# Attention items of three kinds grouped into clusters of every second step, and two qk turns to a bank

## The chip, the cores and the metric

The kernel runs on one core of one Trainium2 chip. The metric is the device time of one execution in microseconds; the median of several runs counts. The engines are named as in the profile: PE is TensorE's matmul stream and PEld its weight loads, DVE is VectorE, ACT is ScalarE, POOL is GpSimd and SP is SyncE, which issues most transfers.

## The reference

The reference is one layer of an encoder over 1024 tokens of width 1024, in float32, with one sequence. Cut to what matters here:

```python
h = rms_norm(x, g_norm1) * (1 + sc1) + sh1          # sc1, sh1, ... from silu(c) @ w_ada
qa, ka, va, qb, kb, vb, gates = split(h @ w_in)     # 8 heads a, 12 heads b, each of 64 columns
qa, ka = rms_norm(qa), rms_norm(ka)                 # per head
o_a = neighbourhood_attention(qa, ka, va, rpb)      # 2-D windows of 8 x 16 on a 16 x 64 grid, with bias
qb, kb = partial_rotary(rms_norm(qb)), partial_rotary(rms_norm(kb))
for g, (win, dil) in enumerate(((128, 1), (512, 4), (2048, 16))):
    o_g, lse_g = dilated_window_attention(qb[g], kb[g], vb[g], win, dil)   # 4 heads each
o_b = sum over g of softmax(lse)_g * o_g
merged = sigmoid(gate_a) * (o_a @ w_proj_a) + sigmoid(gate_b) * (o_b @ w_proj_b)
x = x + gt1 * (merged @ w_o)
x = x + gt2 * swiglu(rms_norm(x, g_norm2) * (1 + sc2) + sh2)               # width 2816
```

A dilated window attends to positions at distances of 0, dil, 2 dil, ... up to win / 2 on either side, so with the tokens sorted by their remainder modulo dil it is a band or a block of a small matrix.

## The kernel before, in words

Each float32 product is made of three float32r matmuls (PASS, L126): the operands are split into a high and a low part, and high by high, high by low and low by high are summed in one bank. PE, ACT, DVE, POOL and SP work at once. The order of PE is the order of the program (the manual schedule for PE near the top of the function); the other engines' instructions are put in order by a planner that simulates the timeline from costs, with a raised priority for functions marked `@urgent` by their offset (PP is 100, QT, AQ, AT and AV are 0). What an instruction must wait for, in banks and tiles too, is worked out by the framework from the accesses.

The input projection and the attention lie in one loop over steps n from 6 to 91 (from L808). A unit is a pair of heads: units 0 and 1 are kind 0 (dilation 1), 2 and 3 kind 1 (dilation 4), 4 and 5 kind 2 (dilation 16), 6 to 9 kind 3 (the neighbourhood). A step is one block of 128 tokens of one unit (n = 8u + t): eight chunks of three matmuls with 384 columns each (proj_chunk, L292) sum q, k and v of that block into a bank of tag d. Then proj_post (L304 to L343) normalises: ACT squares and copies (L310, L311, L327 or L330), DVE reduces and scales (L313 to L315 with rstd at L118 to L123), POOL rotates (L322 to L325). From step 80 on the chunks are those of the gates (L599).

Between the fourth and the fifth chunk of a step stands its block of attention, for older tokens and units, in this order on PE:

- at_scores (L441): the scores of the items that are due, in two banks of tag s, one for each head; six matmuls an item, the two heads on the two halves of the array's rows. at_qk (L455, L456) then reduces on DVE with the mask added and the maximum taken, and ACT makes the exponentials P.
- at_pv (L482): the results of the items of two steps ago, from the turned P and v, into one bank of tag v. DVE copies them out (L485) and SP sends them to DRAM (L486).
- qk_turn (L350): the tokens of two steps ago are transposed, q and k each 128 x 128, into one bank of tag v (s for n under 10). ACT makes the high parts from it (L368 of q, L369 of k), DVE the low parts (L370 of q, L371 of k).
- at_turn (L467): P of the items of the step before is transposed, one bank of tag t for each head; ACT copies one (L473), DVE the other (L471).

There are four tags (t, v, d, s) with two banks of 128 x 512 float32 each. An item is up to 128 queries of one unit with one to three blocks of 128 keys: kind 0 has nine items (the first and the last with 64 queries and one block, the others with two blocks), kind 1 eight with two blocks, kind 2 eight with one, kind 3 eight with two or three. unit_items (L396) lists them with a slot; the loop puts an item of unit u - 1 on step 8u + 2 + slot (the dictionary ready), so that a step has one item, and two where kind 0's last two share slot 7. Such a step's items pass through the same pairs of banks one after the other.

Other work lies in the steps: ada_step (L279, L281, and L258 once in eight steps) for the second half of the modulation, t_piece (L640 to L646), the weight splits (L107 on ACT, L108 on POOL or DVE). After unit 5 the statistics are read back (combine_stats at step 61) and the three dilations are merged (combine_step, L559). The late gate products (gate_prod, L953 and L954 among its evacuations) come after the loop, then the output projection and the feed-forward (L1192, L1362).

Big tiles (4 KB a partition: v, wa2, rb, tp, oacc, gsig, w1m and the landing tiles of the start) share seven places.

Of the kernel before, what the change touches and what calls it, by code (L numbers as in the profile page):

```python
# [10 lines left out]
F32 = mybir.dt.float32  # L11
# [23 lines left out]
WARM = 40  # L35
XSQ = "avavaaaa"
# [5 lines left out]
def hybrid_layer(ctx: ExitStack, tc: tile.TileContext, x, colp, wada1, wada2, bada2, wqkv, wg, wpa, wpb,  # L42
# [95 lines left out]
    NBIG = 7  # L138
# [5 lines left out]
    land = [big("land") for _ in range(NBIG)]  # L144
    seq = [0]

    def landing():
        seq[0] += 1
        return land[(seq[0] - 1) % NBIG]

# [87 lines left out]
    def rope_tab():  # L238
        cs = ap_.tile([128, 4, 64], F32, tag="qn", bufs=5, name="cs").rearrange("p h (a b) -> p (h a) b", b=32)
# [64 lines left out]
    def proj_post(U, t):  # L304
        pd = U.pd[t]
        qn = ap_.tile([128, 4, 64], F32, tag="qn", bufs=5, name="qn")
# [39 lines left out]
    def qk_turn(U, t, tag="v"):  # L346
        qf = U.qn[t].rearrange("p h d -> p (h d)")
        pt = bank(tag)
# [47 lines left out]
    def unit_items(U):  # L396
# [48 lines left out]
    def at_qk(I, h):  # L445
# [3 lines left out]
        P = I.P[h] = ap_.tile([128, 384], F32, tag="p", bufs=4, name="P")  # L449
# [12 lines left out]
    def at_turn(I, h):  # L462
# [5 lines left out]
        PT = I.PT[h] = ap_.tile([128, 3, 128], F32, tag="pT", bufs=3, name="PT")  # L468
# [7 lines left out]
    def at_pv(I):  # L476
# [10 lines left out]
        if I.last:  # L487
            unit_out(U)

# [179 lines left out]
    def ada_rows(k):  # L669
# [10 lines left out]
        def copy():  # L680
            rowk[k] = ap_.tile([128, 384], F32, tag="p", bufs=4, name="rowk")[:, :256]
            nc.scalar.activation(rowk[k], pa[:, :256], AF.Copy)
# [122 lines left out]
    cur, prev, done = [], [], []  # L805
    raws = {}
    nextw = {}
    for n in range(6, 92):  # L808
# [24 lines left out]
        done, prev, cur = prev, cur, ready.pop(n, [])  # L833
# [692 lines left out]
```

## Time and profile before

Three runs took 1538.08, 1543.08 and 1542.0 us, a median of 1542.0. The profiled execution took 1540.34 us, of which the span that the trace shows is 1538.5.

| stretch of the span, us | what | PE busy, us | DVE busy, us | granted clock |
|---|---|---|---|---|
| 69 to 79.5 | steps 8 and 9 | 8.76 | 7.86 | 1.00 |
| 79.5 to 382 | steps 10 to 57, items of kinds 0 to 2 | 295.68 | 221.76 | 0.99 |
| 382 to 540 | steps 58 to 81, kind 3 | 153.89 | 138.83 | 1.00 |
| 540 to 640 | gates, the last items | 100.00 | 49.86 | 1.00 |
| 640 to the end | gates, merge, output projection, feed-forward | 889.69 | 641.22 | 1.00 |

To read the profile: a row of a group has the line, the engine, the operation, the tiles that it writes and reads, and the number of instructions. In a timeline the first column is the start and the second the time from that start to the end of the last of the merged instructions, in us; matmuls overlap in the pipeline, so their starts tell more than their lengths. In a list of waits stand the total, the number of times and the longest. In a row of a stretch stand its length, each engine's busy time with its instructions, the granted clock as a share of full speed, the busy share of the DMA engines and GB/s.

### The profile page before, as it was taken

How to read it: one execution, taken by the hardware profiler on the slowest of the kernel's cores; microseconds unless marked ns; L12 is line 12 of the kernel's file. 1: busy time of each engine (PE TensorE's matmuls, PEld its weight loads, DVE VectorE, ACT ScalarE, POOL GpSimd, SP SyncE). 2: the span in 40 equal slices, each digit the busy share in tenths (PEclk: the TensorE clock that was granted, in tenths of full speed). 3: DMA queues.
4: the chain of work that ended last, by engine and by line, in shares of the span. 5: the costliest groups of instructions: out<-in, count | busy, mean ns of one | idle time of the engine just before them, and what ended most of it. 6: DMA issues, size and time to landing. Idle time of an engine off the chain costs nothing. (4 is left out here: it accounts for less than half of the span.)

```text
span 1538.5 us, 24632 instructions
## 1 busy us (share of the span) xinstructions
PE 1513.6 (98%) x8156; PEld 1268.2 (82%) x8156; DVE 1109.3 (72%) x2428; ACT 671.3 (44%) x1719; POOL 531.8 (35%) x540
## 2 busy tenths in 40 slices
PE   9999999999999999999999999999999999999998
PEld 7988898988888877788888888888888888887886
DVE  6867786776889855466665497788767775599468
ACT  5555654555555453245532344233233333344442
POOL 0422331321000030001361211677777775104464
PEclk9999999999999999999999999999999999999999
DMA  9615355552354354833553235345443334798342
GB/s 366 231 47 177 106 160 163 172 170 83 104 149 131 107 172 138 299 120 117 171 169 139 86 105 179 112 135 178 156 132 103 107 111 131 256 357 284 104 151 103
DMA packets 158016, 241.67 MB, mean 157 GB/s; under 512 B 27312, under 2 KB 77360, under 8 KB 157120
## 3 DMA queue, kind: packets, MB, share of 16 engines
q1 hardware_dynamic: 156736, 235.90, 47.0%
q10 hardware_dynamic: 1152, 4.19, 0.7%
q8 instruction: 65, 1.06, 0.3%
q14 instruction: 63, 0.52, 0.1%
HBM read 179.89 MB, written 60.15 MB: 156 GB/s over the span
## 5 line engine op out<-in xcount | busy, mean ns | idle before, releaser
L107 ACT ACTIVATE whi<-raw 128x512 fp32r<-128x512 f32 (+1 forms) x348 | 205.0, 601 | 300.5 <-PE ps_s L1362 40.6
L108 POOL TENSOR_TENSOR wlo<-raw,whi 128x512 fp32r<-128x512 f32 (+2 forms) x133 | 168.9, 1282 | 473.1 <-ACT whi L107 323.8
L292 PE MATMUL ps_d<-whi,hT 128*128 128x384 f32 x1152 | 317.5, 343 | 1.3 <-ACT v L327 1.3
L108 DVE TENSOR_TENSOR wlo<-raw,whi 128x512 fp32r<-128x512 f32 (+1 forms) x215 | 184.3, 868 | 79.3 <-ACT whi L107 74.6
L292 PEld LDWEIGHTS ps_d<-whi,hT 128*128 128x128 f32 x1152 | 211.0, 188 | 7.0 <-ACT vs L330 2.6
L292 PE MATMUL ps_d<-wlo,hT 128*128 128x384 f32 x576 | 193.9, 337 | 0.4 <-POOL wlo L108 0.4
L292 PEld LDWEIGHTS ps_d<-wlo,hT 128*128 128x128 f32 x576 | 108.8, 189 | 0.7 <-POOL wlo L108 0.7
L107 ACT ACTIVATE whi<-ws 128x512 fp32r<-128x512 f32 x65 | 41.0, 631 | 123.9 <-DVE ws L1209 47.4
L1142 POOL TENSOR_TENSOR e<-e,c 128x512 f32<-128x512 f32 x44 | 68.2, 1549 | 66.3 <-DVE c L1272 40.3
L322 POOL TENSOR_TENSOR ra<-qn,rtab 128x64 f32<-128x64 f32 x48 | 16.8, 349 | 170.8 <-DVE qn L315 144.0
L456 ACT ACTIVATE P<-P,st 128x256 f32<-128x256 f32 (+2 forms) x100 | 46.1, 462 | 58.5 <-DVE st L455 58.5
L108 POOL TENSOR_TENSOR wlo<-m,whi 128x512 fp32r<-128x512 f32 x35 | 51.9, 1493 | 54.6 <-ACT whi L107 54.5
L599 PE MATMUL ps_d<-hT,whi 128*128 128x512 f32 x192 | 60.5, 396 | 0.0
L1192 PE MATMUL ps_v<-h2T,whi 128*128 128x512 f32 x192 | 59.3, 390 | 0.0
L1192 PE MATMUL ps_s<-h2T,whi 128*128 128x512 f32 x192 | 59.2, 390 | 0.0
L456 ACT ACTIVATE P<-P,sx 128x384 f32<-128x384 f32 (+1 forms) x64 | 37.1, 580 | 48.0 <-DVE sx L455 48.0
L441 PE MATMUL ps_s<-qk 64*128 64x256 f32 (+3 forms) x492 | 53.8, 321 | 3.3 <-DVE qk L371 2.0
L1192 PE MATMUL ps_d<-h2T,whi 128*128 128x512 f32 x184 | 56.9, 390 | 0.0
L313 DVE TENSOR_REDUCE ss<-sq 128x4 f32<-128x256 f32 x80 | 33.1, 414 | 32.6 <-ACT sq L310 32.5
L441 PEld LDWEIGHTS ps_s<-qk 64*128 64x128 f32 (+1 forms) x492 | 35.0, 182 | 25.2 <-issue 13.2
L482 PE MATMUL ps_v<-PT,v 128*64 128x128 f32 (+1 forms) x672 | 54.6, 284 | 0.8 <-DVE PT L471 0.8
L108 DVE TENSOR_TENSOR wlo<-ws,whi 128x512 fp32r<-128x512 f32 x45 | 49.4, 1098 | 8.2 <-ACT whi L107 8.2
(436 smaller groups left out, 3989.6 us busy)
## 6 DMA issues: line engine op xcount, KB each, us to landing
raw<-in_w_dram SPq DMA_DIRECT2D x139, 256.0 KB
ga_d<-e SPq DMA_DIRECT2D x77, 256.0 KB
raw<-ga_d SPq DMA_DIRECT2D x77, 256.0 KB
wa<-in_wada_dram SPq DMA_DIRECT2D x32, 512.0 KB
raw<-in_wqkv_dram SPq DMA_DIRECT2D x80, 192.0 KB
m<-in_w_dram SPq DMA_DIRECT2D x44, 256.0 KB
raw<-in_wg_dram SPq DMA_DIRECT2D x42, 256.0 KB
xt<-in_x_dram SPq DMA_DIRECT2D x16, 512.0 KB
```

The source lines that it names most:

```text
L107: nc.scalar.activation(hi[:, :n], r, AF.Copy)
L108: (eng or nc.gpsimd).tensor_sub(lo[:, :n], r, fview(hi[:, :n]))
L292: nc.tensor.matmul(pd[:, :384], tok(a, k, t), U.w[k][b][:, :384], start=(k == 0 and i == 0), stop=(k == KT - 1 and i == 2))
L313: nc.vector.tensor_reduce(ss, sq.rearrange("p (h d) -> p h d", h=4), axis=mybir.AxisListType.X, op=ALU.add)
L322: nc.gpsimd.tensor_tensor(v4(ra), v4(qn[:, :, 0:16]), tv(0, 0, 16), op=ALU.mult)
L441: nc.tensor.matmul(I.pS[h][:nq, :nk], U.qk[a][hs, I.q0:I.q0 + nq], U.qk[2 + b][hs, I.kb0 * 128:I.kb0 * 128 + nk], start=(i == 0), stop=(i ...
L456: nc.scalar.activation(P[:nq, :nk], P[:nq, :nk], AF.Exp, scale=-1.0, bias=nm, accum_out=sm)
L482: nc.tensor.matmul(po[hs, :nq], U.v[:, I.kb0 + i, hs], I.PT[h][:, i, :nq], start=(i == 0), stop=(i == nkb - 1))
L599: nc.tensor.matmul(st["p"], gw[i, br][j][a][:, kk * 128:(kk + 1) * 128], hT[b][:, k, hs], start=(k == 0 and q == 0), stop=(k == 7 and q == 2))
L1142: nc.gpsimd.tensor_mul(sg, sg, up)
L1192: nc.tensor.matmul(pb, w[p][:, k * 128:(k + 1) * 128], b[q][:, k], start=(k == 0 and i == 0), stop=(k == 3 and i == 2))
```

## The change

Up to step 57 (PAIRED is 58) the block of attention is made at odd steps only; the even steps have nothing but their projection. Items of kinds 0 to 2 no longer have a step of their own: they go into a list, and each odd step from 11 on takes from its head as many as have 512 keys together, over the border between two units too, as a Cluster. All scores of a cluster are written first, one item beside the other into the same two banks (cl_scores), then reduced and exponentiated item by item (cl_qk). One odd step later its P are transposed into one bank for each head and copied out in as few pieces as lie together (cl_turn); another odd step later all results go into one bank, are copied once and sent with one transfer for each unit (cl_pv). There are 50 such items and 21 clusters, at the odd steps from 11 to 47 and at 51 and 53.

The qk turns come two to an odd step, of the tokens of three and two steps ago. The two tiles of such a pair share one bank, the first in columns 0 to 255 and the second in columns 256 to 511, and qk_turn is called for the first and then for the second. Tiles of unit 0 are turned at steps 8, 9, 11 and 13. From step 58 on each step is as before.

For this there are seven tiles qn instead of five, four turned P instead of three, wider tiles for P, turned P and staging, and an eighth big tile (the landing tiles stay seven); the reserve for transfer descriptors is set to 1024 bytes a partition. The diff, without the changed sizes of rope_tab, proj_post, at_qk and the start:

```diff
+PAIRED = 58
-    NBIG = 7
+    NBIG, NLAND = 8, 7
-    land = [big("land") for _ in range(NBIG)]
+    land = [big("land") for _ in range(NLAND)]
-        return land[(seq[0] - 1) % NBIG]
+        return land[(seq[0] - 1) % NLAND]
...
-    def qk_turn(U, t, tag="v"):
+    def qk_turn(U, t, tag="v", pt=None):
-        pt = bank(tag)
+        if pt is None:
+            pt = bank(tag)
...
+            I.o = o
...
-        PT = I.PT[h] = ap_.tile([128, 3, 128], F32, tag="pT", bufs=3, name="PT")
+        PT = I.PT[h] = ap_.tile([128, 4, 128], F32, tag="pT", bufs=4, name="PT")
...
         nc.sync.dma_start(I.dst, st[:, :nq])
         if I.last:
             unit_out(U)
+    class Cluster:
+        def __init__(self):
+            self.items, self.keys = [], 0
+        def add(self, I):
+            I.c0 = self.keys
+            self.items.append(I)
+            self.keys += I.nkb * 128
+    def cl_scores(C):
+        C.pS = [bank("s") for _ in range(2)]
+        for I in C.items:
+            U, nq, nk = I.U, I.nq, I.nkb * 128
+            for i, (a, b) in enumerate(PASS):
+                for h in range(2):
+                    hs = slice(h * 64, h * 64 + 64)
+                    nc.tensor.matmul(C.pS[h][:nq, I.c0:I.c0 + nk], U.qk[a][hs, I.q0:I.q0 + nq],
+                                     U.qk[2 + b][hs, I.kb0 * 128:I.kb0 * 128 + nk], start=(i == 0), stop=(i == 2))
+    @urgent(AQ)
+    def cl_qk(C):
+        C.P = [ap_.tile([128, 512], F32, tag="p", bufs=4, name="P") for _ in range(2)]
+        for I in C.items:
+            nq, c = I.nq, slice(I.c0, I.c0 + I.nkb * 128)
+            for h in range(2):
+                nm, sm = I.U.st[:nq, I.item, h:h + 1], I.U.st[:nq, I.item, 2 + h:3 + h]
+                nc.vector.tensor_tensor_reduce(C.P[h][:nq, c], C.pS[h][:nq, c], I.masks[h], -1.0, 3.0e38,
+                                               ALU.add, ALU.min, nm)
+                nc.scalar.activation(C.P[h][:nq, c], C.P[h][:nq, c], AF.Exp, scale=-1.0, bias=nm, accum_out=sm)
+    @urgent(AT)
+    def cl_turn(C):
+        C.PT = []
+        for h in range(2):
+            pt = bank("t")
+            PT = ap_.tile([128, 4, 128], F32, tag="pT", bufs=4, name="PT").rearrange("p b q -> p (b q)")
+            C.PT.append(PT)
+            cuts = []
+            for I in C.items:
+                for i in range(I.nkb):
+                    c = I.c0 + i * 128
+                    nc.tensor.transpose(pt[:, c:c + I.nq], C.P[h][:I.nq, c:c + 128], ident[:I.nq, :I.nq])
+                    if cuts and cuts[-1][1] == c:
+                        cuts[-1][1] = c + I.nq
+                    else:
+                        cuts.append([c, c + I.nq])
+            for a, b in cuts:
+                if h:
+                    nc.vector.tensor_copy(PT[:, a:b], pt[:, a:b])
+                else:
+                    nc.scalar.activation(PT[:, a:b], pt[:, a:b], AF.Copy)
+    @urgent(AV)
+    def cl_pv(C):
+        po = bank("v")
+        n, outs = 0, []
+        for I in C.items:
+            U, nq = I.U, I.nq
+            for i in range(I.nkb):
+                for h in range(2):
+                    hs, c = slice(h * 64, h * 64 + 64), I.c0 + i * 128
+                    nc.tensor.matmul(po[hs, n:n + nq], U.v[:, I.kb0 + i, hs], C.PT[h][:, c:c + nq],
+                                     start=(i == 0), stop=(i == I.nkb - 1))
+            if outs and outs[-1][0] is I.o:
+                outs[-1][3] = n + nq
+            else:
+                outs.append([I.o, I.q0, n, n + nq])
+            n += nq
+        st = ap_.tile([128, 512], F32, tag="stg", bufs=3, name="stg")
+        nc.vector.tensor_copy(st[:, :n], po[:, :n])
+        for o, q0, a, b in outs:
+            nc.sync.dma_start(o[:, q0:q0 + b - a], st[:, a:b])
+        for I in C.items:
+            if I.last:
+                unit_out(I.U)
     def unit_out(U):
         if U.kind == 3:
...
-                ready.setdefault(8 * u + 2 + slot, []).append(I)
+                if I.U.kind < 3:
+                    waiting.append(I)
+                else:
+                    ready.setdefault(8 * u + 2 + slot, []).append(I)
-        done, prev, cur = prev, cur, ready.pop(n, [])
+        if n >= PAIRED:
+            done, prev, cur = prev, cur, ready.pop(n, [])
+        elif n % 2:
+            done, prev, cur = prev, cur, []
+            if waiting:
+                cur = [Cluster()]
+                while waiting and cur[0].keys + waiting[0].nkb * 128 <= 512:
+                    cur[0].add(waiting.pop(0))
+        else:
+            done = []
...
-        turns = [(units[0], tt) for tt in {8: (0, 1), 9: (2, 3), 10: (4,), 11: (5,), 12: (6,), 13: (7,)}.get(n, ())]
-        if 10 <= n <= 81:
-            turns.append((units[(n - 2) // 8], (n - 2) % 8))
+        turns = [(units[0], tt) for tt in {8: (0, 1), 9: (2, 3), 11: (4, 5), 13: (6, 7)}.get(n, ())]
+        if PAIRED <= n <= 81 or 9 < n < PAIRED and n % 2:
+            turns += [(units[m // 8], m % 8) for m in ((n - 2,) if n >= PAIRED else (n - 3, n - 2)) if m >= 8]
...
-        for I in cur:
-            at_scores(I)
-            at_qk(I, 0)
-            at_qk(I, 1)
-        for I in done:
-            at_pv(I)
-        for q in turns:
-            qk_turn(*q, "s" if n < 10 else "v")
-        for I in prev:
-            at_turn(I, 0)
-            at_turn(I, 1)
+        if n >= PAIRED or n % 2 or n < 10:
+            for I in cur:
+                if I.__class__ is Cluster:
+                    cl_scores(I)
+                    cl_qk(I)
+                else:
+                    at_scores(I)
+                    at_qk(I, 0)
+                    at_qk(I, 1)
+            for I in done:
+                (cl_pv if I.__class__ is Cluster else at_pv)(I)
+            for j, q in enumerate(turns):
+                if j % 2 == 0:
+                    pq = bank("s" if n < 10 else "v")
+                qk_turn(*q, "v", pq[:, 256 * (j % 2):256 * (j % 2) + 256])
+            for I in prev:
+                if I.__class__ is Cluster:
+                    cl_turn(I)
+                else:
+                    at_turn(I, 0)
+                    at_turn(I, 1)
...
-    nc = _bacc.Bacc("TRN2", target_bir_lowering=False, num_devices=1)
+    nc = _bacc.Bacc("TRN2", target_bir_lowering=False, num_devices=1, dynamic_dma_scratch_size=1024)
```

More of the change, by code (lines that the diff above doesn't have):

```diff
@@ L238, in rope_tab @@
     def rope_tab():
-        cs = ap_.tile([128, 4, 64], F32, tag="qn", bufs=5, name="cs").rearrange("p h (a b) -> p (h a) b", b=32)
+        cs = ap_.tile([128, 4, 64], F32, tag="qn", bufs=7, name="cs").rearrange("p h (a b) -> p (h a) b", b=32)
         nc.sync.dma_start(cs, rope)
@@ L305, in proj_post @@
         pd = U.pd[t]
-        qn = ap_.tile([128, 4, 64], F32, tag="qn", bufs=5, name="qn")
+        qn = ap_.tile([128, 4, 64], F32, tag="qn", bufs=7, name="qn")
         U.qn[t] = qn
@@ L448, in at_qk @@
         pS = I.pS[h]
-        P = I.P[h] = ap_.tile([128, 384], F32, tag="p", bufs=4, name="P")
+        P = I.P[h] = ap_.tile([128, 512], F32, tag="p", bufs=4, name="P")
         if U.kind < 3:
@@ L680, in copy @@
         def copy():
-            rowk[k] = ap_.tile([128, 384], F32, tag="p", bufs=4, name="rowk")[:, :256]
+            rowk[k] = ap_.tile([128, 512], F32, tag="p", bufs=4, name="rowk")[:, :256]
             nc.scalar.activation(rowk[k], pa[:, :256], AF.Copy)
@@ L805, in hybrid_layer @@
     cur, prev, done = [], [], []
+    waiting = []
     raws = {}
```

## The prediction

> **What bounds the kernel now.** I read the page first, for the engine that has no room left.
>
> ```profile
> span 1538.5 us, 24632 instructions
> PE 1513.6 (98%) x8156; PEld 1268.2 (82%) x8156; DVE 1109.3 (72%) x2428; ACT 671.3 (44%) x1719; POOL 531.8 (35%) x540
> ```
>
> PE is busy for 98% of the span, so time is won or lost only where PE's own stream becomes shorter or longer. A measurement of this kernel can tell some 0.3% from no change, 4.6 us.
>
> Then the busy time by stretch: the steps 10 to 57, which the change regroups, run from 79.5 us to about 383 us, the steps 8 and 9 just before.
>
> ```profile
> core 0: us, PE busy (x) PEld busy (x) DVE busy (x) ACT busy (x) POOL busy (x), PEclk, DMA share, GB/s
> 79.50:382.00 302.50, 295.68 (x2027) 262.36 (x2028) 221.76 (x792) 171.26 (x647) 80.08 (x193) 0.99 0.44 134
> ```
>
> Here too PE is the bound (295.68 of 302.50 us). The waits of PE from 69 to 382 us show how little idleness there is to take away:
>
> ```profile
> PE ps_s L441 <- DVE qk L371: 2.0, 1, 2.0
> PE ps_d L292 <- ACT v L327: 1.3, 1, 1.3
> PE ps_s L441 <- DVE st L455: 1.2, 2, 0.6
> PE ps_t L467 <- ACT PT L473: 0.9, 2, 0.5
> PE ps_v L482 <- DVE PT L471: 0.8, 2, 0.4
> ```
>
> What is left is how PE strings its instructions together. The timeline of PE around one block of attention in the middle of a step, and a later block with three key blocks:
>
> ```profile
> 158.76 0.33 PE L292 MATMUL ps_d<-wlo,hT 128*128 128x384 f32 x1
> 158.94 0.34 PE L292 MATMUL ps_d<-whi,hT 128*128 128x384 f32 x1
> 159.21 0.62 PE L441 MATMUL ps_s<-qk 64*128 64x256 f32 x6
> 159.76 0.66 PE L482 MATMUL ps_v<-PT,v 128*64 128x128 f32 x8
> 160.34 0.44 PE L350 MATMUL ps_v<-ident,qn 128*128 128x128 f32 x2
> 160.62 0.60 PE L467 MATMUL ps_t<-ident,P 128*128 128x128 f32 x4
> 160.98 0.43 PE L292 MATMUL ps_d<-whi,hT 128*128 128x384 f32 x1
> 161.24 0.34 PE L292 MATMUL ps_d<-wlo,hT 128*128 128x384 f32 x1
> ...
> 428.34 0.88 PE L482 MATMUL ps_v<-PT,v 128*64 128x128 f32 x12
> 429.15 0.44 PE L350 MATMUL ps_v<-ident,qn 128*128 128x128 f32 x2
> 429.42 0.82 PE L467 MATMUL ps_t<-ident,P 128*128 128x128 f32 x6
> 430.00 0.43 PE L292 MATMUL ps_d<-whi,hT 128*128 128x384 f32 x1
> ```
>
> Matmuls overlap, so the distance of the starts counts. A projection matmul takes 0.18 us (158.76 to 158.94). The block takes 161.24 - 158.94 = 2.30, less two such distances (0.35): 1.95 us.
>
> **Term 1: half as many blocks.** The number of PE instructions stays the same; 48 blocks (steps 10 to 57) become 24. A second item in a block costs only its marginal price. Results: 12 matmuls take 0.81 (428.34 to 429.15) where 8 take 0.58, so eight more cost 0.46. Turns of P: six take 0.58 where four take 0.36, so 0.11 each, 0.44 for four; the two transposes of a second qk turn 0.22 at the same price. Six more scores: no row shows two items back to back in one bank; between 0.35 (the 0.058 of a result matmul, which also runs in pairs on half the array) and the full 0.55 (159.21 to 159.76). I take 0.35, because the block's entry is in the 0.55. Sum 1.47, so a double block takes 3.42 against 3.90 and each pair of steps gains 0.48: 24 x 0.48 = 11.5 us (with 0.55 for the scores 6.7). Items of kind 2 have one key block each; I let them gain the same.
>
> **Term 2: waits that lose their reason.** In the steps with two items of kind 0 the second item waits for banks that the first still holds (L455 1.2, the turned P 0.9 + 0.8); in clusters they share the bank. The 2.0 us is a unit's first scores behind its last qk turn one step earlier; now two steps lie between. Together 4.9 us. That longest wait also cost clock:
>
> ```profile
> 238.00:243.00 5.00, 3.04 (x22) 2.52 (x21) 4.64 (x16) 2.21 (x6) 0.00 (x0) 0.80 0.09 26
> 243.00:249.00 6.00, 6.00 (x39) 5.45 (x38) 4.25 (x18) 2.43 (x11) 1.74 (x7) 0.88 0.91 240
> ```
>
> The lost part is 0.20 x 5 + 0.12 x 6 = 1.7 us. Next late after them would be the projection's bank (L292 behind L327, 1.3), which the change leaves. I take 7 us, between 3 and 9.
>
> **Term 3: a wait that is new.** The qk turns now go two to a bank: the transposes of tile a into columns 0 to 255, then ScalarE (L368, L369) and VectorE (L370, L371) read them, and only then, in program order, come the transposes of tile b into columns 256 to 511. In the kernel before every turn has a bank for itself, so no row shows PE writing one half while another engine reads the other. The nearest rows are those of readers. L370 needs what L368 wrote and reads columns 0 to 127; L369 reads columns 128 to 255 and its result is nothing to L370. Yet L370 waits for it (the tile qk, 69 to 382 us, what it was released by and who waited):
>
> ```profile
>   ACT qk L369: 6.2, 15
> ...
>   DVE qk L370: 6.7, 16
> ```
>
> A second place is the late gate products, where L954 copies a bank into its own half of a tile and uses nothing that L953 made, but L953 reads the same bank:
>
> ```profile
> L954 ACT ACTIVATE sg<-ps_t x1: 601/601/601, 711.7 to 711.7; 128x512 f32<-128x512 f32 x1
> ...
>   DVE sg L953: 1.4, 1
> ```
>
> So in this program two engines at one bank are ordered even when their columns differ and both only read. A write by PE into a bank that is being read should be no freer: tile b's transposes wait until L371 of tile a has ended. The Trainium skill ("PSUM — Partial Sum Buffer", section "PSUM bank collisions raise a hardware error") says that engines must be kept apart by bank and quadrant of partitions and not by address. By that rule the wait is there and the sum is the one below; by addresses alone it is that of the first rival. The two rows agree with the rule; that PE's writes obey it too no run here shows yet.
>
> The size of the wait, from when tile b's transposes could start (0.28 after tile a's, 160.34 to 160.62) to the end of L371, in three steps of before:
>
> ```profile
> 162.64 0.28 DVE L371 TENSOR_TENSOR qk<-ps_v,qk 128x128 fp32r<-128x128 f32 x1
> 248.84 0.44 PE L350 MATMUL ps_v<-ident,qn 128*128 128x128 f32 x2
> 249.75 0.42 DVE L471 COPY PT<-ps_t 128x256 f32<-128x256 f32 x1 [0.41 <-PE ps_t L467]
> 250.35 0.28 DVE L371 TENSOR_TENSOR qk<-ps_v,qk 128x128 fp32r<-128x128 f32 x1
> 274.60 0.44 PE L350 MATMUL ps_v<-ident,qn 128*128 128x128 f32 x2
> 277.47 0.27 DVE L371 TENSOR_TENSOR qk<-ps_v,qk 128x128 fp32r<-128x128 f32 x1
> ```
>
> 162.92 - 160.34 - 0.28 = 2.30; 250.63 - 248.84 - 0.28 = 1.51; 277.74 - 274.60 - 0.28 = 2.86. The mean is 2.2. I take 2.0, because the copy of the turned P (L471, 0.42) that VectorE makes ahead of L371 in the second of these steps can't be there: PE reaches the turns of P only after this wait. Against a smaller value, VectorE has four score reductions before the turn where it had two. The ends for the range are 1.1 (the shortest less that copy) and 2.9 (the longest). Queued behind the waiting transposes are the turns of P of the cluster before, the second half of the step's projection and all of the next step's, and behind those ScalarE's squares of the projection. Nothing covers it, since PE is the bound.
>
> How often: the 56 tiles of units 0 to 6 make 28 pairs (steps 8 and 9 one each, 11 and 13 two each, 15 to 57 one in each of 22 odd steps). 28 x 2.0 = 56 us.
>
> Waits of this length can also cost clock. The 2.0 us idle at 240 us was followed by the 0.80 and 0.88 above; an idle of 1.7 us later was not:
>
> ```profile
> L559 PE MATMUL ps_t<-ident,fb 128*128 128x128 f32 x4 | 0.7, 287 | 1.7 <-ACT PT L473 1.7
> 434.00:438.00 4.00, 3.90 (x34) 3.50 (x34) 3.17 (x14) 1.34 (x7) 0.00 (x0) 1.00 0.60 166
> ```
>
> I let two of the 28 do so: 2 x 1.7 = 3.4 us. The Trainium skill ("TensorE: Matmul & The Clock Gate", Part 1, on the HAM clock gate) has the clock halved after an idle window of some 3.4 us, and the window free-running. The 2.0 us shows that less idleness can do it here; the third rival is where it does so often.
>
> **At nothing.** The score reductions and exponentials come in fours instead of twos; their results are needed a pair of steps later, so the projection in between hides them, and what could be exposed (VectorE's queue ahead of L370) is in term 3's ends. Copies of turned P and of results become fewer and wider on engines that are not the bound (VectorE 221.76 of 302.50). The result transfers leave SP in fewer pieces and up to a pair of steps later, but unit 5's last results come at step 57 instead of 59, before the statistics are read at step 61, and no transfer stands in PE's waits. The eighth big tile, seven qn tiles, the wider P, PT and staging tiles and the smaller descriptor reserve move addresses, not work. If smaller reserves slowed transfers, weight splits would come late; the DMA share of 0.44 leaves room for that.
>
> **Sum.** Against the profiled execution (1540.34 us, its span 1538.5): 1540.3 - 11.5 - 7 + 56 + 3.4 = 1581.2. That execution lies 1.7 us under the median of 1542.0, so 1583 us.
>
> **Rivals.** (1) The halves of a bank are independent for PE: tile b's transposes go on at once, and terms 1 and 2 stand alone: 1540.3 - 18.5 + 1.7 = 1523.5. For it: no row shows PE itself held back that way; against it, L370's 16 waits and L954's. This is the faster side. (2) The wait exists but is nearly covered: it pays back terms 1 and 2 at 18.5 / 28 = 0.66 us a pair, 1542. For it: the planner that orders ScalarE and VectorE may put the four reads first; against it, the shortest of the three is 1.51, and 1.1 without the copy. (3) The waits are longer and half of them halve the clock: 28 x 2.4 = 67, 14 x 1.7 = 24, so 1540.3 - 18.5 + 67 + 24 + 1.7 = 1614.5. For it: the 2.0 us at 240 did; against it: 1.7 us at 434 did not.
>
> **Chances.** Forecast 0.72, for waits of 1.1 to 2.9 us (28 x 1.1 = 31 with term 2 at 9 and no clock lost gives 1552.5, 28 x 2.9 = 81 with terms 1 and 2 at 6.7 and 3 gives 1617); rival 1 0.10; rival 2 0.05, split 0.02 faster, 0.02 same, 0.01 slower; rival 3 0.13. So faster 0.12, same 0.02, slower 0.86. The range holds the forecast's ends and the middle of rival 3, and leaves out rivals 1 and 2 and the longer half of rival 3: 1553 to 1620.
>
> **What would show it.** Right: in the list of PE's waits a new largest entry, L350 behind L371, some 28 times for about 56 us, and PE busy clearly under 98%; a block of two items 3.4 us long apart from that wait; L441 behind L371 and behind L455 gone; granted clock under 1.00 in a few windows. Wrong: no such entry (rival 1), or one of less than 0.7 us each (rival 2). A long new wait of PE elsewhere, on transfers for instance, would mean that I looked at the wrong place.

## The result, and the profile after

The changed kernel takes 1624.88 us, the median of six runs (1618.99 to 1627.43), against 1540.41 for the kernel before, also of six (1537.82 to 1543.08). The ratio is 1.055, with a 95% interval from 1.0532 to 1.0567. The direction and the mechanism are those of the prediction, but the time lies 42 us above 1583 and just beyond the upper end of the range, 1620.

The profiled execution took 1627.35 us. By the change the lines have moved: the projection is L293, the transposes of a qk turn L352, ScalarE's two reads of them L370 and L371, VectorE's two L372 and L373. In the clusters L511 are the scores, L521 and L523 the reductions and exponentials, L536 the turns of P, L556 the results and L564 their copy. From the page, the span, the busy time, the granted clock in 40 slices and two groups:

```profile
span 1625.5 us, 24441 instructions
PE 1538.7 (95%) x8156; PEld 1301.9 (80%) x8156; DVE 1109.7 (68%) x2374; ACT 670.8 (41%) x1694; POOL 532.2 (33%) x540
PEclk9989898998999999999999999999999999999999
...
L293 PE MATMUL ps_d<-whi,hT 128*128 128x384 f32 x1152 | 329.9, 359 | 0.0
...
L352 PE MATMUL ps_v<-ident,qn 128*128 128x128 f32 x152 | 35.0, 317 | 66.9 <-DVE qk L373 53.6
```

PE makes the same 8156 matmuls but is busy 25.1 us longer (1513.6 before), and its idle time has grown too, from 24.9 to 86.8 us. So there are two losses, PE waiting and PE working more slowly. The first third of the clock row dips below 9 several times. The idle time stands ahead of the transposes of the qk turn (66.9 us). By stretches, first the steps 8 to 57 (which took 315.50 us before, with 306.93 busy) and then all the rest:

```profile
core 0: us, PE busy (x) PEld busy (x) DVE busy (x) ACT busy (x) POOL busy (x), PEclk, DMA share, GB/s
68.20:472.80 404.60, 332.85 (x2105) 306.50 (x2104) 231.16 (x783) 180.61 (x646) 86.26 (x212) 0.89 0.35 109
472.80:1625.50 1152.70, 1141.24 (x5567) 937.14 (x5565) 829.73 (x1451) 450.04 (x942) 434.93 (x301) 1.00 0.47 153
```

All of the loss lies in the steps that were regrouped, 89.1 us. The rest took 1154.90 us before. From here on "the stage" means the steps 8 to 57. PE's waits in it, with the total, the number and the longest:

```profile
PE ps_v L352 <- DVE qk L373: 53.6, 21, 6.2
PE ps_v L352 <- POOL rb L325: 8.8, 3, 3.0
PE ps_v L352 <- POOL qn L326: 4.6, 2, 2.6
PE ps_s L352 <- DVE qk L373: 4.5, 2, 2.6
```

The four rows are the 28 waits between the two tiles of a pair, 71.5 us. Five of them are put down to POOL, whose instruction happened to end last. It belonged to the rotation of a later tile: counted in order, tile b's own rotation (L326) had ended 2.6 us or more before PE went on, in all 24 pairs that have one. In the instructions of all 28 PE starts again 0.06 to 0.15 us after the end of L373. One of these five, in the timeline of PE, ScalarE and VectorE:

```profile
225.82 0.49 ACT L523 ACTIVATE P<-P,st 128x256 f32<-128x256 f32 x1
225.99 0.44 PE L352 MATMUL ps_v<-ident,qn 128*128 128x128 f32 x2
226.29 0.41 DVE L564 COPY stg<-ps_v 128x256 f32<-128x256 f32 x1
226.31 0.39 ACT L523 ACTIVATE P<-P,st 64x128 f32<-64x128 f32 x1
...
226.70 0.49 ACT L523 ACTIVATE P<-P,st 128x256 f32<-128x256 f32 x1
...
227.19 0.35 ACT L370 ACTIVATE qk<-ps_v,hg 128x128 fp32r<-128x128 f32 x1
227.44 0.26 ACT L371 ACTIVATE qk<-ps_v 128x128 fp32r<-128x128 f32 x1
227.73 0.35 DVE L372 SCALAR_TENSOR_TENSOR qk<-ps_v,hg,qk 128x128 fp32r<-128x128 f32 x1 [0.51 <-ACT qk L371]
228.00 0.28 DVE L373 TENSOR_TENSOR qk<-ps_v,qk 128x128 fp32r<-128x128 f32 x1
...
228.42 0.41 PE L352 MATMUL ps_v<-ident,qn 128*128 128x128 f32 x2 [1.99 <-POOL qn L326]
```

Tile a is transposed by 226.43. ScalarE is still at the exponentials of the block's own scores and comes to L370 at 227.19. VectorE has been through its reductions and a copy, waits for L371, and L373 ends at 228.28. Then tile b is transposed. Over the 28 waits (1.30 to 6.17 us, median 2.19, mean 2.55) the parts are, in the mean: 1.00 us until ScalarE begins L370, 0.56 for L370 and L371, 0.30 until VectorE begins L372, 0.57 for L372 and L373, 0.12 until PE goes on. In the longest, 6.17 us, VectorE began L372 3.24 us late, because work ahead of it on its queue (L282, L721) waited for transfers.

The slower work is seen in the stretches ahead of and behind two waits, each 3.41 us:

```profile
211.73:215.14 3.41, 1.62 (x13) 1.66 (x14) 1.55 (x8) 2.73 (x12) 0.00 (x0) 1.00 0.29 47
215.14:218.56 3.42, 3.42 (x22) 3.42 (x21) 1.29 (x5) 2.13 (x6) 0.00 (x0) 1.00 0.90 239
225.39:228.80 3.41, 1.42 (x20) 1.04 (x15) 2.34 (x12) 2.27 (x10) 1.05 (x4) 1.00 0.93 256
228.80:232.22 3.42, 3.42 (x16) 3.42 (x15) 1.89 (x5) 1.13 (x3) 0.00 (x0) 0.50 1.09 379
```

The wait of 1.82 us in the first row (1.79 of it inside the row) left the clock alone; the one of 1.99 in the third was followed by 3.4 us at half clock, in which PE made 16 matmuls where the second row has 22. The record of the granted clock has 17 such stretches in the stage, of 3.4 or 6.8 us, 92 us together; before it had one of 3.4.

### The profile page after: what moved, and what is told of

The parts are those of the page before. It is cut to its first block, busy times and chain, and to the rows that moved or that the text cites. A ratio compares the mean times of both kernels' runs of the same rounds, so it can differ in the third digit from the quotient of the medians.

```text
span 1625.5 us, 24441 instructions
## 1 busy us (share of the span) xinstructions
PE 1538.7 (95%) x8156; PEld 1301.9 (80%) x8156; DVE 1109.7 (68%) x2374; ACT 670.8 (41%) x1694; POOL 532.2 (33%) x540
## 5 line engine op out<-in xcount | busy, mean ns | idle before, releaser
L109 POOL TENSOR_TENSOR wlo<-raw,whi 128x512 fp32r<-128x512 f32 (+2 forms) x133 | 174.3, 1320 | 501.7 <-ACT whi L108 316.8
L293 PE MATMUL ps_d<-whi,hT 128*128 128x384 f32 x1152 | 329.9, 359 | 0.0
L293 PEld LDWEIGHTS ps_d<-whi,hT 128*128 128x128 f32 x1152 | 227.3, 203 | 5.2 <-issue 2.6
L293 PE MATMUL ps_d<-wlo,hT 128*128 128x384 f32 x576 | 203.7, 354 | 0.4 <-POOL wlo L109 0.4
L293 PEld LDWEIGHTS ps_d<-wlo,hT 128*128 128x128 f32 x576 | 117.0, 203 | 0.7 <-POOL wlo L109 0.7
L352 PE MATMUL ps_v<-ident,qn 128*128 128x128 f32 x152 | 35.0, 317 | 66.9 <-DVE qk L373 53.6
L352 PEld LDWEIGHTS ps_v<-ident,qn 128*128 128x128 f32 x152 | 16.3, 150 | 80.5 <-issue 42.3
L311 ACT ACTIVATE sq<-ps_d 128x256 f32<-128x256 f32 x74 | 28.2, 382 | 112.7 <-PE ps_d L293 109.7
L523 ACT ACTIVATE P<-P,st 128x256 f32<-128x256 f32 (+2 forms) x100 | 45.3, 455 | 41.8 <-DVE st L521 41.8
L1244 ACT ACTIVATE e<-e 128x512 f32<-128x512 f32 x44 | 27.4, 630 | 72.5 <-DVE e L1379 47.2
```

Source lines behind the costliest of these rows:

```text
L109: (eng or nc.gpsimd).tensor_sub(lo[:, :n], r, fview(hi[:, :n]))
L293: nc.tensor.matmul(pd[:, :384], tok(a, k, t), U.w[k][b][:, :384], start=(k == 0 and i == 0), stop=(k == KT - 1 and i == 2))
L311: nc.scalar.activation(sq, pd[:, :256], AF.Square)
L352: nc.tensor.transpose(pt[:, i * 128:(i + 1) * 128], qf[:, i * 128:(i + 1) * 128], ident)
L523: nc.scalar.activation(C.P[h][:nq, c], C.P[h][:nq, c], AF.Exp, scale=-1.0, bias=nm, accum_out=sm)
```

## The experiments

Theory at this point: PE is made to wait with tile b while anything still reads tile a in the same bank; that wait is 2.55 us long 28 times, and its idleness halves the clock after most of them. The rivals were that the clusters themselves (wider tiles, fours of reductions, the smaller reserve) cost something, and that the order on ScalarE, not the bank, makes the wait as long as it is. Each experiment was timed beside the kernel before on the same chip (medians of 1534.93 to 1537.54 us), so ratios are compared. "Idle" is the length of the stage less PE's busy time in its row, "slower" is that busy time less that of the first experiment, whose matmuls are the same.

### Both tiles transposed before either is read

qk_turn is called in two parts, for the transposes and for the four reads.

```diff
-            for j, q in enumerate(turns):
-                if j % 2 == 0:
-                    pq = bank("s" if n < 10 else "v")
-                qk_turn(*q, "v", pq[:, 256 * (j % 2):256 * (j % 2) + 256])
+            for j in range(0, len(turns), 2):
+                pq = bank("s" if n < 10 else "v")
+                for part in ("write", "read"):
+                    for i, q in enumerate(turns[j:j + 2]):
+                        qk_turn(*q, "v", pq[:, 256 * i:256 * i + 256], part)
```

> The changed kernel with one thing altered: of each pair of qk turns both tiles are transposed before either is read, still in one shared bank. Theory (the loss is PE waiting for tile a's four reads before it may write tile b's columns, and the half clock that follows): L352 behind L373 vanishes from PE's waits (56.5 us in the changed kernel), the granted clock of 69 to 471 us goes from 0.89 to 0.99 or more, and terms 1 and 2 stand alone: 1519 to 1528 us. Rival (the clusters themselves, their later scores and their bursts on VectorE, cost the time): PE's waits move to other lines and the time stays above 1590 us.

Measured: 1522.50 us against 1534.93, 0.9918 (0.9903 to 0.9932), as expected. The bank is still shared; only the order has changed. Its busy time, its stage, and PE around a full block:

```profile
PE 1500.1 (99%) x8156; PEld 1269.1 (83%) x8156; DVE 1101.4 (72%) x2374; ACT 666.5 (44%) x1694; POOL 536.8 (35%) x540
```

```profile
67.90:365.20 297.30, 293.27 (x2104) 272.25 (x2104) 224.94 (x780) 172.71 (x645) 91.85 (x211) 0.99 0.47 145
```

```profile
217.90 0.34 PE L293 MATMUL ps_d<-whi,hT 128*128 128x384 f32 x1
218.17 0.98 PE L514 MATMUL ps_s<-qk 64*128 64x256 f32 x12
219.08 1.09 PE L559 MATMUL ps_v<-PT,v 128*64 128x128 f32 x16
220.10 0.66 PE L353 MATMUL ps_v<-ident,qn 128*128 128x128 f32 x4
220.60 1.04 PE L539 MATMUL ps_t<-ident,P 128*128 128x128 f32 x8
221.39 0.42 PE L293 MATMUL ps_d<-whi,hT 128*128 128x384 f32 x1
221.65 0.33 PE L293 MATMUL ps_d<-wlo,hT 128*128 128x384 f32 x1
```

The four transposes go in one piece (L353 here), and the idle time of the stage is 4.0 us. So the wait is a matter of order, not of sharing. This version beats both kernels. Against it the loss of the changed kernel divides: the stage is 404.60 - 297.30 = 107.3 us longer, of which 67.7 is idle time (71.75 against 4.03) and 39.6 slower work (332.85 against 293.27).

### One part alone: paired turns without clusters, clusters without paired turns

The first puts each item back on its own step and keeps two turns to a bank; the second keeps the clusters and gives each turn its own step and bank.

```diff
-        if n >= PAIRED:
-            done, prev, cur = prev, cur, ready.pop(n, [])
...
+        done, prev, cur = prev, cur, ready.pop(n, [])
```

> The changed kernel without clusters: every item has its own step and its own banks as in the kernel before, and only the qk turns come in pairs that share a bank, at odd steps. Theory: the same 28 waits and half clocks without what the clusters gain, so 1630 to 1650 us, slower than the changed kernel by 10 to 20 us. Rival (the clusters cost the time): within 10 us of the kernel before.

```diff
-        if PAIRED <= n <= 81 or 9 < n < PAIRED and n % 2:
-            turns += [(units[m // 8], m % 8) for m in ((n - 2,) if n >= PAIRED else (n - 3, n - 2)) if m >= 8]
+        if 10 <= n <= 81:
+            turns.append((units[(n - 2) // 8], (n - 2) % 8))
...
-                qk_turn(*q, "v", pq[:, 256 * (j % 2):256 * (j % 2) + 256])
+                qk_turn(*q, "s" if n < 10 else "v")
```

> The changed kernel with the clusters, but each qk turn in its own step and with a bank of its own, as in the kernel before. Theory: no wait of PE behind L373, and most of the gain of the clusters less the turns' separate places at even steps: 1524 to 1536 us. Rival (the clusters, or the wider tiles and the smaller descriptor reserve, cost the time): above 1590 us.

Measured: pairs alone 1618.19, 1.0541 (1.0526 to 1.0557), below the 1630 to 1650 that was expected; clusters alone 1524.98, 0.9928 (0.9912 to 0.9945), as expected. Pairs alone, the two largest rows of PE's waits between the tiles of a pair, and the stage:

```profile
PE ps_v L352 <- DVE qk L373: 46.1, 24, 3.7
PE ps_s L352 <- DVE qk L373: 6.1, 2, 3.5
```

```profile
68.10:464.60 396.50, 335.43 (x2093) 296.72 (x2092) 230.46 (x819) 184.40 (x669) 85.67 (x211) 0.93 0.36 112
```

The pairs bring a loss of the same size (1.0541 against 1.055) without any cluster: idle 61.1 us, and 28.5 of slower work against the kernel before (335.43 against 306.93). It is less than was expected of them, because their 28 waits are shorter: 2.03 us in the mean against 2.55, with 0.35 against 1.00 until ScalarE begins L370. The clusters cost nothing and bring nearly all of the gain that the first experiment shows. That rival is out.

### The wait filled with work of no use

Twenty transposes of the identity, into a bank that nothing reads, stand between the two tiles of a pair.

```diff
                 if j % 2 == 0:
                     pq = bank("s" if n < 10 else "v")
+                elif n < PAIRED:
+                    pf = bank("t")
+                    for i in range(20):
+                        nc.tensor.transpose(pf[:, :128], ident, ident)
```

> The changed kernel with 20 more transposes of the identity (0.11 us each at full clock, 2.2 us) between the first and the second tile of each pair, into a bank that nothing reads: PE is kept busy while it would wait. Theory that idleness halves the clock and that this is the larger part of what the prediction missed: the granted clock of the steps 8 to 57 rises from 0.89 to 0.98 or more, the wait before L352 shrinks to below 20 us in all, and although 560 transposes are added the time falls to 1590 to 1612 us. Rival (the clock costs nothing that the waits do not cost already): 1625 us or more.

Measured: 1596.83, 1.0402 (1.0387 to 1.0418), as expected. Its stage:

```profile
67.80:444.40 376.60, 359.60 (x2665) 336.05 (x2664) 230.79 (x782) 180.33 (x646) 86.95 (x211) 0.99 0.38 117
```

The 560 fillers start 0.109 us apart, 61 us in all, and 17.0 us are still idle: 78 us in which PE does nothing for the result, more than the 71.75 of the changed kernel. Yet the stage is 28.0 us shorter. What has gone is slower work, 359.60 - 61 - 293.27 = 5.3 us instead of 39.6. So idleness, and not the transposes or the bank, costs the clock.

### A raised priority for the turns

```diff
-PP, QT, AQ, AT, AV = 100, 0, 0, 0, 0
+PP, QT, AQ, AT, AV = 100, 100, 0, 0, 0
```

> The changed kernel with the qk turns' instructions raised in the planner's priority to that of the projection's (QT from 0 to 100), so that ScalarE and VectorE read tile a ahead of the cluster's exponentials and copies. Theory (the wait is 2.55 us and not 2.0 because up to four exponentials stand ahead of L370 on ScalarE): the 28 waits shrink to 1.4 to 1.9 us each, fewer of them halve the clock, and the time falls to 1570 to 1605 us. Rival (the wait is the chain of the four reads itself): 1615 us or more.

Measured: 1621.08, 1.0538 (1.0522 to 1.0554). The expectation failed. The 28 waits are in the mean what they were (2.55 us, with 0.99 until ScalarE begins L370), because the order on ScalarE is the same: the exponentials still stand ahead of L370. Why the raised priority did not move them, no run shows.

### The same order, a bank for each tile

```diff
-            for j, q in enumerate(turns):
-                if j % 2 == 0:
-                    pq = bank("s" if n < 10 else "v")
-                qk_turn(*q, "v", pq[:, 256 * (j % 2):256 * (j % 2) + 256])
+            for q in turns:
+                qk_turn(*q, "s" if n < 10 else "v")
```

> The changed kernel, its order on PE unchanged, but the two tiles of a pair each take the next bank of tag v, as every turn did in the kernel before. Theory (the bank is what is waited for): L352 no longer waits for L373; in its place tile b waits for VectorE's copy of the cluster's results out of the other v bank (L564), some 0.4 to 0.9 us, 22 times: 1530 to 1548 us, granted clock 0.99 or more. Rival (the order of the two tiles on PE costs it, whatever the banks): above 1600 us.

Measured: 1575.34, 1.0239 (1.022 to 1.0259), between the two expectations. PE's longest waits and the stage:

```profile
PE ps_v L352 <- DVE stg L564: 36.4, 19, 4.7
PE ps_v L352 <- DVE qk L373: 5.0, 2, 3.5
```

```profile
68.00:421.00 353.00, 308.94 (x2103) 283.73 (x2103) 229.56 (x782) 177.82 (x646) 88.36 (x211) 0.95 0.40 123
```

The wait on L373 goes (the two that are left are the steps with four tiles for two banks), and another takes its place: tag v has two banks, the results of the cluster (L556) fill one just before tile a takes the other, so tile b needs the bank that VectorE still has to copy out (L564). It is 1.9 us long, 19 times, not the 0.4 to 0.9 that was expected.

### Work of use put into the wait

First the turns of P go between the two tiles; then those and three chunks of the projection, for 24 of the 28 pairs.

```diff
                 if j % 2 == 0:
                     pq = bank("s" if n < 10 else "v")
+                else:
+                    p_turns()
                 qk_turn(*q, "v", pq[:, 256 * (j % 2):256 * (j % 2) + 256])
```

> The changed kernel with the turns of P of the cluster before moved between the two tiles of the pair. Theory: 0.8 us of useful work cover a part of each wait, so the 28 waits keep 1.5 to 1.9 us of idleness in all but the longest, and idleness of that length halves the clock only sometimes: 1560 to 1595 us. Rival (any wait at this place halves the clock, whatever its length): above 1600 us.

```diff
+                if j % 2 and n > 9 and (n > 13 or j == 3):
+                    late.append((q, half))
...
         chunk()
         chunk()
         chunk()
+        if n > 9 and n % 2 and n < PAIRED:
+            for q, half in late:
+                qk_turn(*q, "v", half)
         chunk()
```

> The changed kernel with the turns of P and three chunks of the projection (0.8 and 1.6 us) between the two tiles of the pair, for 24 of the 28 pairs; the shared bank and the order of writing and reading stay. Theory (a wait costs only what is not covered): what remains are the 4 pairs of the steps 8 to 13 and the longest of the others, 10 to 20 us, so 1528 to 1550 us and a granted clock of 0.97 or more in the steps 8 to 57. Rival (the sharing costs by itself, by the array's or the bank's own slowness): above 1590 us.

Measured: 1593.29, 1.0362 (1.0344 to 1.038), and 1550.71, 1.009 (1.0063 to 1.0117), the one near the end of what was expected and the other just above it. The two stages:

```profile
68.00:440.10 372.10, 312.30 (x2104) 286.79 (x2103) 229.17 (x783) 179.71 (x646) 87.08 (x212) 0.94 0.38 117
```

```profile
67.90:400.50 332.60, 303.26 (x2105) 277.01 (x2104) 225.40 (x781) 176.12 (x646) 90.43 (x212) 0.97 0.42 130
```

With the turns of P between, the idle time is 59.8 us, 12.0 less than in the changed kernel, and the slower work 19.0 us, 20.6 less: waits that are a sixth shorter halve the loss of clock. With the projection as well 29.3 and 10.0 us are left, where 10 to 20 us of waiting were expected. Covering the wait helps as far as it reaches; the order of the first experiment needs no cover.

### The readers put first on their queues

First ScalarE's exponentials are pinned behind L370 and L371, then VectorE's score reductions behind L372 and L373 too. (pin keeps the order of the program on its engine; the exponentials in cl_qk have it as well.)

```diff
-        nc.scalar.activation(qh, qs, AF.Identity, scale=g)
-        nc.scalar.activation(kh, ks, AF.Copy)
+        pin(nc.scalar.activation(qh, qs, AF.Identity, scale=g))
+        pin(nc.scalar.activation(kh, ks, AF.Copy))
...
                     cl_scores(I)
-                    cl_qk(I)
...
                 qk_turn(*q, "v", pq[:, 256 * (j % 2):256 * (j % 2) + 256])
+            for I in cur:
+                if I.__class__ is Cluster:
+                    cl_qk(I)
```

> The changed kernel with the order of ScalarE alone altered: each cluster's exponentials are held behind the reads of the qk turns (L370, L371) instead of three of four standing ahead of them; PE's order and the shared banks stay. Theory (of the mean wait of 2.55 us in the changed kernel 1.0 is ScalarE's queue ahead of L370, the rest the four reads, VectorE's queue and the restart): the 28 waits shrink to 1.5 to 1.8 us each, 42 to 50 us in all, the time at half clock falls from 92 us to 20 to 60, and the time is 1568 to 1592 us. Rival (raising the priority changed nothing because the wait doesn't come from ScalarE's queue): 1610 us or more.

```diff
-        nc.vector.scalar_tensor_tensor(ql, qs, g, fview(qh), op0=ALU.mult, op1=ALU.subtract)
-        nc.vector.tensor_sub(kl, ks, fview(kh))
+        pin(nc.vector.scalar_tensor_tensor(ql, qs, g, fview(qh), op0=ALU.mult, op1=ALU.subtract))
+        pin(nc.vector.tensor_sub(kl, ks, fview(kh)))
...
-                nc.vector.tensor_tensor_reduce(C.P[h][:nq, c], C.pS[h][:nq, c], I.masks[h], -1.0, 3.0e38,
+                pin(nc.vector.tensor_tensor_reduce(C.P[h][:nq, c], C.pS[h][:nq, c], I.masks[h], -1.0, 3.0e38,
```

> As with the exponentials behind the qk turns, and VectorE's score reductions of the cluster held behind L372 and L373 as well, so that neither engine has work of the cluster ahead of the reads of tile a. Theory (ScalarE's and VectorE's queues stood side by side, and with ScalarE's taken away VectorE's took its place: 0.94 us in the mean instead of 0.30): both gone, most of the 28 waits come down to the chain of the four reads, 1.3 to 1.6 us, 38 to 48 us in all, and the time to 1562 to 1590 us. Rival (something else on the way, POOL's rotation of the second tile or the clock, holds the wait at over 2 us): 1605 us or more.

Measured: 1615.08, 1.0481 (1.0438 to 1.0524), and 1592.69, 1.0348 (1.0305 to 1.039). One wait of the first of the two, in the timeline:

```profile
189.52 0.27 ACT L371 ACTIVATE qk<-ps_v 128x128 fp32r<-128x128 f32 x1
...
190.38 0.42 DVE L521 CUSTOM_DVE_ANT_0 P<-ps_s,bmask 128x256 f32<-128x256 f32 x1
...
191.06 0.42 DVE L564 COPY stg<-ps_v 128x256 f32<-128x256 f32 x1
191.40 0.34 DVE L372 SCALAR_TENSOR_TENSOR qk<-ps_v,hg,qk 128x128 fp32r<-128x128 f32 x1
191.66 0.28 DVE L373 TENSOR_TENSOR qk<-ps_v,qk 128x128 fp32r<-128x128 f32 x1
192.09 0.45 PE L352 MATMUL ps_v<-ident,qn 128*128 128x128 f32 x1 [2.87 <-POOL rb L325]
```

And one of the second:

```profile
196.53 0.27 ACT L371 ACTIVATE qk<-ps_v 128x128 fp32r<-128x128 f32 x1
196.83 0.35 DVE L372 SCALAR_TENSOR_TENSOR qk<-ps_v,hg,qk 128x128 fp32r<-128x128 f32 x1 [0.50 <-ACT qk L371]
197.10 0.28 DVE L373 TENSOR_TENSOR qk<-ps_v,qk 128x128 fp32r<-128x128 f32 x1
197.53 0.41 PE L352 MATMUL ps_v<-ident,qn 128*128 128x128 f32 x2 [1.30 <-DVE qk L373]
```

In the first, ScalarE is done with L371 at 189.79, but VectorE is at four score reductions and the copy of the results and begins L372 only at 191.40. In the mean the delay at ScalarE falls from 1.00 to 0.20 us and that at VectorE rises from 0.30 to 0.94, so the wait is still 2.38 and the expectation failed. The second came out just above its own. With the exponentials and the reductions behind the reads, ten of the 28 waits are at 1.30 us or just below, the bare chain of the four reads (0.53 and 0.55, with 0.03 to 0.15 around them), and the mean is 1.94. So the two queues stood side by side, and clearing one only uncovered the other. The queues are not empty even now: ScalarE is 0.13 us late in the mean and VectorE 0.57, behind work that was not moved (L282, L316, L564, L721). In the longest wait, 5.48 us, VectorE stands at L721 until a transfer has landed, with L372 queued behind:

```profile
332.54 0.69 DVE L721 TENSOR_TENSOR tp<-tp 128x512 f32<-128x512 f32 x1 [4.08 <-DMA tp<-h_d]
333.15 0.34 DVE L372 SCALAR_TENSOR_TENSOR qk<-ps_v,hg,qk 128x128 fp32r<-128x128 f32 x1
```

Even so the kernel is 3.5% slower than the kernel before, and 4.3% slower than with both tiles first (1.0348 against 0.9918).

### All together

| kernel | stage, us | idle | slower | at half clock | ratio |
|---|---|---|---|---|---|
| the change | 404.6 | 71.8 | 39.6 | 92 | 1.055 |
| raised priority | 398.5 | 71.9 | 33.4 | 75 | 1.0538 |
| exponentials behind | 394.2 | 68.4 | 32.5 | 72 | 1.0481 |
| turns of P between | 372.1 | 59.8 | 19.0 | 41 | 1.0362 |
| reductions behind too | 370.6 | 54.7 | 22.6 | 44 | 1.0348 |
| a bank for each | 353.0 | 44.1 | 15.7 | 34 | 1.0239 |
| projection between | 332.6 | 29.3 | 10.0 | 20 | 1.009 |
| both tiles first | 297.3 | 4.0 | 0 | 3.4 | 0.9918 |

In each row with waits the slower work is 0.43 to 0.51 of the time at half clock, and 0.32 to 0.55 of the idle time. The four columns in the middle are from one profiled execution each, and the executions of one kernel differ: the granted clock was 0.971 in the profiled one of the changed kernel and 0.973 to 0.976 in its other five, and 0.992 against 0.996 to 0.998 with the projection between. So small differences between two rows say little.

## Why the prediction was wrong, point by point

**The bound** held: PE sets the time of the stage, and what came onto its path came into the time whole.

**Term 1** (24 blocks x 0.48 = 11.5 us) held in the price of a block. A full block of two items and two turns takes 221.65 - 217.90 - 0.35 = 3.40 us without the wait, where the prediction has 3.42, and the parts fit too: scores 0.91, results 1.02, a double turn 0.50, turns of P 0.79.

**Term 2** (7 us) is no longer found in the waits: the scores' waits behind the last qk turn and behind the other item are gone from PE's list. Terms 1 and 2 together, 18.5 us, come out as 18.2 from the profiles (315.5 to 297.3) but as 12.4 from the times side by side (1534.93 to 1522.50, by the interval 10 to 15). The profiled execution of the kernel before, 1540.34 us, is slower than the kernel before was on that chip, so the second number counts. From the profiles PE's busy time in the stage fell by 13.7 us (306.93 to 293.27) and its idle time by 4.5 (8.57 to 4.03), where term 1 has 11.5 and the waits of term 2 have 4.9. The 1.7 us of clock in term 2 did not come: the kernel before and the first experiment each have one stretch of 3.4 us at half clock. Where the 5.8 us between 18.2 and 12.4 lie, no run shows, since no profile of the kernel before was taken beside the first experiment.

**Term 3, that there is a wait,** held: 28 times, L352 behind L373, and gone when the order alone is changed (the first experiment). The Trainium skill's rule that engines are kept apart by bank and quadrant, whatever the columns ("PSUM — Partial Sum Buffer", section "PSUM bank collisions raise a hardware error"), was cited with the remark that no run showed it for PE's writes. In these runs PE goes on 0.06 to 0.15 us after the last read of the other half. That is the wait which the framework puts into the program. What the chip would do without it no run shows, nor whether the framework goes by bank or by tile, which are the same here.

**Term 3, its size**: "I take 2.0" a pair. It was 2.55, 71.5 us instead of 56. The step that failed is the dismissal of the queues: I went below the mean of the rows, 2.2, because a copy of the turned P could not be there, and noted the four score reductions only as something against it. The exponentials I counted "at nothing", for their results. They are late for no one, but they stand ahead of L370: ScalarE begins it 1.00 us after PE stops, and 0.20 when they are held behind. VectorE's queue stood beside ScalarE's, so that alone takes only 0.17 off the wait. With the exponentials and the reductions both behind the reads the mean is 1.94 us, near the 2.0 that I took.

**The clock is the step that failed most**: "I let two of the 28 do so: 2 x 1.7 = 3.4 us". Seventeen stretches were at half clock, and they cost 39.6 us. I had one wait of 2.0 us that halved the clock and one of 1.7 that did not, and a forecast of 2.0 for each wait; I should have taken the first row for the rule, since the forecast was at its length; 1.7 us lies in the range where, by the later runs, either can happen. That this is a failure of its own is seen where the waits had the forecast size: with the reductions behind too, 54.7 us were idle and 22.6 us still went to slower work. Summed from the profiled executions: 1627.35 - 1581.2 = 46.1 us too little, of which 36.2 is the clock (39.6 - 3.4), 11.7 the idle time (67.7 - 56), 0.3 terms 1 and 2 (6 by the times side by side), and -2.2 the rest of the span.

**At nothing**: held for the wider tiles and copies, the reserve and the transfers. The clusters alone are 0.7% faster, and the rest of the span is 1152.7 us against 1154.9.

**Rivals.** The first (the halves are independent) and the second (nearly covered) are out. The price of the first, 1523.5, is near what the program gives when the order is right, 1522.5, though partly by chance: the kernel before ran 5.5 us faster on that chip. The third, given 0.13, has the right shape: 28 x 2.4 and half of the waits at half clock, 1614.5. It was 28 x 2.55 and 17 stretches, at 39.6 / 17 = 2.3 us each instead of 1.7, because ten of the 17 were 6.8 us long. It came nearest, and the row that spoke for it, the 2.0 us at 240, stood in the prediction.

**What stays open**: what decides whether idle time of 1.26 to 1.9 us in one window costs clock. That the profiled execution with the raised priority lost 33.4 us of clock and not 39.6 at the same waits shows no difference between the two kernels: both had 17 stretches at half clock, of which five and ten were 6.8 us long, and over all executions the granted clocks overlap (0.975 to 0.977 against 0.971 to 0.976). Where the waits fall against the clock's windows differs by the step and the execution, but no run varied that alone.

## What to carry to other kernels

When two results of PE share a bank, have PE write both before any engine reads either; then sharing cost nothing here, while write, read, write makes PE wait for the whole chain of readers and for whatever stands ahead of them on their queues, an instruction that waits for a transfer included. So cost those queues and not just the reads. A short wait of PE that comes again in every step costs more than its length: in these kernels it cost a further 0.3 to 0.55 us of lost clock for each microsecond of idle time. A raised priority or one cleared queue need not shorten a wait; look at what comes last after it.

## What the runs showed of the hardware

The clock follows idleness far shorter than I had assumed. The half clock comes in stretches of 3.41 or 6.83 us that lie on a fixed grid of 3.41 us. Over the stages of all kernels every window of that grid at full clock with more than 1.9 us of idle time was followed by one; of those with 1.26 to 1.9 us some were (the lowest is 1.26, with the turns of P between) and some were not (up to 1.86, with the projection between). The changed kernel has two windows with 1.82 us, at 82 and at 92 us of the span; only the second was followed. So what counts is how much idle time falls into one window, and between 1.26 and 1.9 us something that these traces do not show decides. A stretch of 6.83 us is one whose own first window had idle time again: 0.75 us or more in the ten long ones of the changed kernel, 0.69 or less in its seven short ones. So a long wait that reaches over the border of two windows, or a second wait soon after, doubles the stretch. The Trainium skill ("TensorE: Matmul & The Clock Gate", Part 1, on the HAM clock gate) gives the window as free-running and some 3.4 us long, which the grid agrees with, and has the clock halved after an idle window; here a window that was idle for about half of its length was enough, and the measurement decides.
